# A hybrid decoder block: eight places for the second half's scores, and 72 instead of 68 first-layer blocks ahead of the dense stage

## The chip, the core and the metric

The kernel runs on one core of a Trainium2 chip. Five engines work side by side, each through its own instructions in a fixed order: TensorE (PE), VectorE (DVE), ScalarE (ACT), GpSimd (POOL) and SyncE (SP), which here only issues transfers. The metric is device microseconds of the whole launch.

## The reference, cut to what matters

A decoder block with two token mixers, followed by a retrieval layer (PEER). Only the last part matters here; `x2` is the normalised result of the mixers, 1024 tokens of width 1024.

```python
q = (xb @ w_q).reshape(TOK_BLOCK, PEER_HEADS, 2, PEER_DHALF)
s = jnp.einsum('thcd,hcnd->thcn', q, sub_keys)
top_s, top_i = lax.top_k(s, K)                      # K = 16 of 128, 8 heads x 2 halves
...                                                 # best 16 of the 256 sums per head
e = (i1 * PEER_NKEYS + i2)                          # 128 experts per token, of 16384
gate = jax.nn.softmax(best_s, axis=-1)
act = jax.nn.gelu(jnp.einsum('td,ted->te', xb, expert_u[e]))
return jnp.einsum('te,ted->td', gate * act, expert_v[e])
```

## The kernel before, in words

The 1024 tokens are eight tiles of 128, worked in two halves of four (tiles 0 to 3, then 4 to 7). The mixers are computed for each half in turn; `mix_and_route(hf, ...)` ends each half: it multiplies by `w_o`, normalises, and routes.

**Routing** runs over 16 pieces `m` (8 heads by 2 key halves). For each, PE multiplies `x2` by one tile of `w_q` (24 matmuls into `acc`, named WQ below), ACT copies the result to `qT`, PE forms the scores against the keys (four matmuls into `sc`, L964), ACT copies the scores to SBUF (L966), and DVE takes the 16 best of each token in place (`top16`, L788 to L792). After every fourth piece `route` picks the 16 best pairs of two heads. In the second half the scores' copies go to three buffers (`sc_s`, pool `sq1`), so a fourth copy waits until DVE has done with the first.

**The retrieval** is done in two ways. Tiles 0 to 2, and the first layer of tile 3, are gathered: for each token's 128 experts POOL issues an indirect load of 128 rows of 8 KB (L1002, 1 MB, called a row load below), DVE forms the dot product (L1005), ACT the gate (L1006, L1007), and DVE adds the weighted second part (L997). There are three row buffers (`NROW`). Tile 0's 128 row loads run beside routing and the stage after it, at a low priority; tiles 1 and 2 (256 row loads) run in the dense stage.

For tiles 4 to 7 all 16384 experts are computed, as 128 blocks of 128 experts, and tile 3 joins in for the second layer. This has three stages:

1. `spread_gates` turns indices and gates into a dense table: 160 steps, each three DVE instructions (L1073, L1076, L1083) and one or two of ACT and POOL that build one-hot operands, and four PE matmuls into `pg` (L1085). The last table pieces go to DRAM (`gd`, L1090).
2. First-layer blocks ahead of time: for each block in `PRE`, `u_stage` loads 512 KB of `expert_u`, splits each half into two parts (ACT the high one `uh`, POOL the low one `ul`; four buffers of each), multiplies with 24 matmuls, and ACT applies the gelu into `g1` (L1098), which is stored to DRAM (`gs`, L1232). `g1` has two buffers (pool `up`). `PRE` holds 68 blocks: every even group of four, and the last two groups. PE does these beside stage 1.
3. `dense`: 32 groups of four blocks. For a block in `PRE` the `g1` is loaded back (L1128); for the others (15 odd groups) `u_stage` runs here. DVE multiplies with the gates (L1131), the product is split into `c2`, and for each half of the output columns 60 matmuls (L228 to L230, five token tiles by four blocks by three) accumulate, and DVE adds the result (L1158: ten additions a group). The loop asks for eight rows of tiles 1 and 2 in every group. `vraw` are the 256 KB loads of `expert_v`, split into `vhi` and `vlo`. The first `c2` buffers lie where `spread_gates` had its table pieces `gt`.

The order of instructions on each engine is set by a scheduler when the program is built, with its own estimates of time and with priorities; a stage's instructions may so be interleaved with another's. On the chip each engine keeps that order and waits on semaphores. "U1" to "U72" below are the first-layer blocks in the order of `PRE`.

Of the kernel before, what the change touches and what calls it, by code (L numbers as in the profile page):

```python
# [10 lines left out]
F32 = mybir.dt.float32  # L11
# [9 lines left out]
P = 128  # L21
# [14 lines left out]
WD = 512 + XD  # L36
DT = list(range(4, 8)) + list(range(NGT, 4))
NG, NQ, GB, NB = WD // GT, 512 // GT, 4, 4
PRE = [b for b in range(128) if b // 4 % 2 == 0 or b >= 120]
NROW = 3  # L40
NV2 = 6
SOONER = 300
# [90 lines left out]
def body(tc, a, out):  # L133
# [3 lines left out]
    def pool(es, name, bufs=1, space=None, side=None):  # L137
        kw = {}
        if space is not None:
            kw["space"] = space  # L140
        if side is not None:
            kw["side"] = side
        return es.enter_context(tc.tile_pool(name=name, bufs=bufs, reuse_waits="tile", **kw))
# [649 lines left out]

    def route(tp, hf, hq, tv, ti, F):

# [5 lines left out]
        for i in range(8):  # L801
# [5 lines left out]
        row = cst[:, C_ROW:C_ROW + 16]  # L807
        V.scalar_tensor_tensor(flat(F)[:, :, 1:], tf.rearrange("p t (h x) k -> p (t h) x k", x=2)[:, :, 0], 8192.0,
                               row[:, None, :].to_broadcast([P, 8, 16]), op0=OP.mult, op1=OP.add)
        dF = tp.tile([P, 8, 16], F32, name="dF")  # L810
        V.tensor_sub(dF, flat(F)[:, :, 1:], flat(F)[:, :, :16])
        bv_ = tp.tile([P, 4, 2, 16], F32, name="bv")
# [37 lines left out]
    def mix_and_route(hf, es, xt):  # L850
        side = "right" if hf else None
        if hf == 0:
            xt = pool(es, "xt0")
            mp = pool(es, "mp0")
        if hf:
            sq = pool(es, "sq1", side=side)
            mp = pool(es, "mp1", side=side)
            sp = pool(es, "sp1", side=side)
            mo = pool(es, "mo1", side=side)
        else:  # L860
            sq = sp = pool(es, "sp0")
            mo = mp
        tp = pool(es, f"tp{hf}", 1, side=side)
        if hf == 0:
# [19 lines left out]
        s2 = loaded(mp, sil, "s2", "s2")  # L884
# [65 lines left out]
            SY.dma_start(hd[t], hb[t])  # L950
        subk = mo.tile([P, 16, P], F32, name="subk", tag="o2") if hf else sp.tile([P, 16, P], F32, name="subk")
        SY.dma_start(subk, a["subk"])
        F = tp.tile([P, 4, 2, 17], F32, name="F")
        V.memset(F, 0.0)
        for m in range(16):
            _, hi, lo = wtile(a["w_q"][m], "wq")
            ps = acc_.tile([P, 512], F32, name="acc")
            for c in range(NCD):
                mm3(ps, hi[:, c], lo[:, c], x2[:, 0, c], x2[:, 1, c], c == 0, c == NCD - 1)
            q = sp.tile([P, 512], F32, name="qT", tag="ld", bufs=3)  # L960
            A.activation(q, ps, AF.Copy)
            p2 = sps.tile([P, 4, P], F32, name="sc")
            for t in range(4):
                PE.matmul(p2[:, t], q[:, t * P:(t + 1) * P], subk[:, m], start=True, stop=True)  # L964
            sc = sq.tile([P, 4, P], F32, name="sc_s", bufs=3 if hf else 4)
            A.activation(sc, p2, AF.Copy)  # L966
            if m % 4 == 0:
                tv = tp.tile([P, 4, 4, 16], F32, name="tv", bufs=2)
                ti = tp.tile([P, 4, 4, 16], U32, name="ti", bufs=2)
            for t in range(4):  # L970
                top16(tv[:, t, m % 4], ti[:, t, m % 4], sc[:, t])
            if m % 4 == 3:
                route(tp, hf, m // 4, tv, ti, F)
        return x2
# [126 lines left out]
    def dense(es, x2, gp, hr, direct, gk1, vr):  # L1101
# [14 lines left out]
        for g0 in range(0, P, NB):  # L1116
            blks = range(g0, g0 + NB)
            cs = []
            for b in blks:
# [5 lines left out]
                g1 = up.tile([P, 512], F32, name="g1")  # L1125
                if b in PRE:
                    act = g1
# [69 lines left out]
    with ExitStack() as e0:  # L1197
        mix_and_route(0, e0, None)
# [28 lines left out]
    with ExitStack() as e0:  # L1227
        spread_gates(e0, direct)
    for b in PRE:
        g1 = up.tile([P, 512], F32, name="g1")  # L1230
# [19 lines left out]
```

## Time and profile before

| | |
|---|---|
| median of 3 runs | 3660.15 us (3648.31 to 3672.93) |
| the profiled execution | 3670.3 us, its span 3668.5 us |
| TensorE's mean granted clock | 0.937 of full |
| busy share of the span | PE 90%, DVE 75%, POOL 64%, ACT 42% |
| DMA | 867.64 MB, mean 237 GB/s |

Busy shares are means over stages with different limits. By the trace, the second half's routing lies at about 1595 to 1875 us, the spreading of the gates at 1875 to 2292, and the dense stage at 2313 to 3647; the last outputs are written by 3668. PE's busy time counts pipelined matmuls that overlap, so a count of matmuls says more.

### The profile page before, as it was taken

What the parts mean: (1) busy time and instruction counts of PE and PEld (TensorE: products, weight loads), DVE (VectorE), ACT (ScalarE), POOL (GpSimd) and SP (SyncE); (2) the same over time, 40 slices, a digit from 0 to 9 for tenths busy, and PEclk for the clock granted to TensorE, in tenths of its full rate; (3) what the DMA queues carried; (4) which work ended last, traced back from release to release, by engine and by line L of the source; (5) the groups of instructions that cost most, each with busy time, mean ns of one, the idle gap of its engine ahead of it and who ended that gap; (6) DMA issues with size and microseconds to landing.
All of it is one profiled execution on the core that took longest, in us unless ns stands there. A gap on an engine that the chain in (4) does not pass through costs nothing. (4 is left out here: it accounts for less than half of the span.)

```text
span 3668.5 us, 49271 instructions
## 1 busy us (share of the span) xinstructions
PE 3313.7 (90%) x16175; PEld 2656.0 (72%) x16175; DVE 2738.7 (75%) x5108; ACT 1554.1 (42%) x3711; POOL 2344.6 (64%) x2123
## 2 busy tenths in 40 slices
PE   7999998889888998788889999789999999999996
PEld 7887776677666775576678888567777787777775
DVE  3566538969986777799999999566766666666776
ACT  5555443243344433333346767433333343333333
POOL 3442304536787646755788999666767676776765
PEclk9999969999898897898999999899999999999998
DMA  4321113333677678863589999888888888988986
GB/s 154 110 65 53 55 44 121 106 133 98 206 219 242 189 224 292 312 235 124 186 288 324 326 331 329 318 303 307 325 306 321 326 314 318 326 327 313 336 324 230
DMA packets 347380, 867.64 MB, mean 237 GB/s; under 512 B 53208, under 2 KB 132704, under 8 KB 293876
## 3 DMA queue, kind: packets, MB, share of 16 engines
q0 software_dynamic: 75328, 475.06, 36.5%
q1 hardware_dynamic: 182436, 328.77, 26.8%
q10 hardware_dynamic: 89360, 60.68, 5.2%
q8 instruction: 127, 2.08, 0.2%
q14 instruction: 129, 1.06, 0.1%
HBM read 777.48 MB, written 86.92 MB: 236 GB/s over the span
## 5 line engine op out<-in xcount | busy, mean ns | idle before, releaser
L1002 POOL DMA_INDIRECT row<-euv,idx x384 | 420.7, 1096 | 318.8 <-DVE yr L997 163.5
L1005 DVE SCALAR_TENSOR_TENSOR row<-row,xr 128x1024 f32<-128x1024 f32 x256 | 311.3, 1217 | 166.7 <-DMA row<-euv,idx 164.9
L225 POOL TENSOR_TENSOR vlo<-vraw,vhi 128x512 fp32r<-128x512 f32 x256 | 330.7, 1303 | 149.0 <-ACT vhi L224 129.3
L997 DVE SCALAR_TENSOR_TENSOR yr<-row,act,yr 128x1024 f32<-128x1024 f32 x256 | 329.5, 1287 | 115.5 <-ACT act L1007 109.8
L1006 ACT ACTIVATE act<-act 128x1 f32<-128x1 f32 x384 | 76.8, 200 | 687.4 <-DVE row L1005 683.6
L225 POOL TENSOR_TENSOR ul<-ur,uh 128x512 fp32r<-128x512 f32 x256 | 344.7, 1353 | 36.4 <-ACT uh L224 27.3
L230 PE MATMUL zp<-x,ul 128*128 128x512 f32 x784 | 314.3, 401 | 16.9 <-POOL ul L225 16.9
L228 PE MATMUL py<-vhi,c 128*128 128x512 f32 x640 | 258.9, 409 | 68.2 <-DVE hbuf L1158 31.6
L228 PE MATMUL zp<-x,uh 128*128 128x512 f32 x784 | 314.9, 402 | 0.3 <-ACT g L1098 0.3
L229 PE MATMUL zp<-x,uh 128*128 128x512 f32 x784 | 313.7, 400 | 0.0
L230 PE MATMUL py<-vhi,c 128*128 128x512 f32 x640 | 254.0, 403 | 23.5 <-POOL c L225 23.5
L224 ACT ACTIVATE vhi<-vraw 128x512 fp32r<-128x512 f32 x256 | 159.6, 626 | 256.8 <-DMA vraw<-euv 110.6
L228 PE MATMUL zp<-vhi,c 128*128 128x512 f32 x640 | 249.5, 399 | 12.0 <-DVE hbuf L1158 10.1
L997 DVE SCALAR_TENSOR_TENSOR hr<-row,act,hr 128x1024 f32<-128x1024 f32 x128 | 235.1, 1837 | 33.8 <-ACT act L1007 33.5
L229 PE MATMUL py<-vlo,c 128*128 128x512 f32 x640 | 256.7, 401 | 0.4 <-POOL vlo L225 0.4
L229 PE MATMUL zp<-vlo,c 128*128 128x512 f32 x640 | 250.1, 395 | 0.4 <-POOL vlo L225 0.4
L230 PE MATMUL zp<-vhi,c 128*128 128x512 f32 x640 | 246.8, 395 | 0.0
L349 DVE SCALAR_TENSOR_TENSOR cy<-u,vec,cy 128x512 f32<-128x512 f32 x240 | 241.9, 1008 | 5.4
L1005 DVE SCALAR_TENSOR_TENSOR row<-row,xng 128x1024 f32<-128x1024 f32 x128 | 213.7, 1672 | 16.0 <-DMA row<-euv,idx 16.0
L1024 POOL DMA_INDIRECT row<-euv,twice x128 | 150.3, 1175 | 114.7 <-DVE row L1026 74.1
L1026 DVE SCALAR_TENSOR_TENSOR row<-row,xng 128x1024 f32<-128x1024 f32 x128 | 184.3, 1445 | 51.9 <-DMA row<-euv,twice 51.7
L228 PEld LDWEIGHTS py<-vhi,c 128*128 128x128 f32 x640 | 124.0, 194 | 110.1 <-DVE hbuf L1158 43.2
(1646 smaller groups left out, 9502.0 us busy)
## 6 DMA issues: line engine op xcount, KB each, us to landing
vraw<-euv SPq DMA_DIRECT2D x256, 256.0 KB
ur<-eut SPq DMA_DIRECT2D x256, 256.0 KB
gd<-gt ACTq DMA_DIRECT2D x20, 1920.0 KB
gblk<-gd SPq DMA_DIRECT2D x30, 1280.0 KB
gs<-g SPq DMA_DIRECT2D x68, 256.0 KB
g<-gs SPq DMA_DIRECT2D x68, 256.0 KB
wbr<-w_in SPq DMA_DIRECT2D x64, 256.0 KB
wqr<-w_q SPq DMA_DIRECT2D x64, 256.0 KB
```

Source lines behind the costliest of these rows:

```text
L224: A.activation(hi, src, AF.Copy)
L225: return eng.tensor_sub(lo, src, hi.bitcast(F32))
L228: PE.matmul(ps, whi, xhi, start=first, stop=False)
L229: PE.matmul(ps, whi, xlo, start=False, stop=False)
L230: PE.matmul(ps, wlo, xhi, start=False, stop=last)
L349: V.scalar_tensor_tensor(y, u[:, j:j + 512], cw, y, op0=OP.mult, op1=OP.add)
L997: V.scalar_tensor_tensor(y, row[:, 1], act[:, j:j + 1], y, op0=OP.mult, op1=OP.add)
L1002: G.indirect_dma_start(out=row.rearrange("p a d -> p (a d)"), out_offset=None, in_=a["euv"], in_offset=bass.IndirectOffsetOnAxis(ap=idx[0] ...
L1005: V.scalar_tensor_tensor(row[:, 0], row[:, 0], 1.0, xn, op0=OP.mult, op1=OP.mult, accum_out=aj)
L1006: A.activation(aj, aj, AF.Gelu)
L1024: G.indirect_dma_start(out=row, out_offset=None, in_=a["euv"].rearrange("e (k d) -> (e k) d", k=2), in_offset=bass.IndirectOffsetOnAxis(ap ...
L1026: V.scalar_tensor_tensor(row, row, 1.0, xn, op0=OP.mult, op1=OP.mult, accum_out=act[:, j:j + 1])
```

## The change

The pool `sq1` with its three buffers goes. In the second half the scores' copies go to `scb`, one tile of eight places in the pool `mp1`, under the tag `s2`: the room of the mixers' operand `s2`, which is no longer read at that time (both are 16 KB a partition). Place `m % 8` is used for piece `m`, so a copy waits for DVE's use of the piece eight before it, not three. And `PRE` takes in the blocks 116 to 119 (group 29): 72 blocks run ahead, 56 remain in the dense stage.

```diff
--- before.py
+++ after.py
@@ -36,7 +36,7 @@
 WD = 512 + XD
 DT = list(range(4, 8)) + list(range(NGT, 4))
 NG, NQ, GB, NB = WD // GT, 512 // GT, 4, 4
-PRE = [b for b in range(128) if b // 4 % 2 == 0 or b >= 120]
+PRE = [b for b in range(128) if b // 4 % 2 == 0 or b >= 116]
 NROW = 3
 NV2 = 6
 SOONER = 300
@@ -853,12 +853,11 @@
             xt = pool(es, "xt0")
             mp = pool(es, "mp0")
         if hf:
-            sq = pool(es, "sq1", side=side)
             mp = pool(es, "mp1", side=side)
             sp = pool(es, "sp1", side=side)
             mo = pool(es, "mo1", side=side)
         else:
-            sq = sp = pool(es, "sp0")
+            sp = pool(es, "sp0")
             mo = mp
         tp = pool(es, f"tp{hf}", 1, side=side)
         if hf == 0:
@@ -950,6 +949,7 @@
             SY.dma_start(hd[t], hb[t])
         subk = mo.tile([P, 16, P], F32, name="subk", tag="o2") if hf else sp.tile([P, 16, P], F32, name="subk")
         SY.dma_start(subk, a["subk"])
+        scb = mp.tile([P, 8, 4, P], F32, name="scb", tag="s2") if hf else None
         F = tp.tile([P, 4, 2, 17], F32, name="F")
         V.memset(F, 0.0)
         for m in range(16):
@@ -962,7 +962,7 @@
             p2 = sps.tile([P, 4, P], F32, name="sc")
             for t in range(4):
                 PE.matmul(p2[:, t], q[:, t * P:(t + 1) * P], subk[:, m], start=True, stop=True)
-            sc = sq.tile([P, 4, P], F32, name="sc_s", bufs=3 if hf else 4)
+            sc = scb[:, m % 8] if hf else sp.tile([P, 4, P], F32, name="sc_s", bufs=4)
             A.activation(sc, p2, AF.Copy)
             if m % 4 == 0:
                 tv = tp.tile([P, 4, 4, 16], F32, name="tv", bufs=2)
```

The scheduler makes a new order of the whole second half from this. Three places of it follow.

ACT, second half of routing, before: from the thirteenth score copy (L966) to the fifteenth. `uh` are splits of first-layer weights, `g1` gelus of finished first-layer blocks, `act` the gathered rows' gates.

```order
L966 ACTIVATE sc_s_13873<-sc_13868 128x512
L224 ACTIVATE uh_17762<-ur_17760 128x512
L1098 ACTIVATE g1_17673<-zp_17686 128x512
L224 ACTIVATE uh_17796<-ur_17794 128x512
L224 ACTIVATE uh_17802<-ur_17800 128x512
L1098 ACTIVATE g1_17713<-zp_17726 128x512
L224 ACTIVATE uh_17836<-ur_17834 128x512
L966 ACTIVATE sc_s_13941<-sc_13936 128x512
L224 ACTIVATE uh_17842<-ur_17840 128x512
L1098 ACTIVATE g1_17753<-zp_17766 128x512
L1006 ACTIVATE act_14400<-act_14400 128x1
L966 ACTIVATE sc_s_14007<-sc_14002 128x512
```

The same copies (thirteenth to fifteenth) in the new order, and the sixteenth behind them; `wqh` and `qT` belong to WQ, `bf` to `route`.

```order
L966 ACTIVATE scb_12750<-sc_13854 128x512
L224 ACTIVATE uh_17617<-ur_17615 128x512
L966 ACTIVATE scb_12750<-sc_13921 128x512
L224 ACTIVATE uh_17623<-ur_17621 128x512
L961 ACTIVATE qT_13984<-acc_13959 128x512
L224 ACTIVATE uh_17657<-ur_17655 128x512
L844 ACTIVATE bf_13454<-bf_13454 128x128
L224 ACTIVATE uh_17663<-ur_17661 128x512
L961 ACTIVATE qT_14049<-acc_14024 128x512
L966 ACTIVATE scb_12750<-sc_13986 128x512
L224 ACTIVATE uh_17697<-ur_17695 128x512
L966 ACTIVATE scb_12750<-sc_14051 128x512
```

The last four copies moved ahead of every gelu (L1098) of a first-layer block; before, three of them stand behind one.

DVE, the end of `spread_gates`, before: the last two steps of three instructions, the last row of tile 0 (`hr0`), its final normalisation (L199 to L1039), and the first product of the dense stage (L1131).

```order
L1073 TENSOR_TENSOR o2h_17600<-gT1_17159,keys_15203 128x512
L1076 TENSOR_TENSOR o1h_17602<-gT0_17151,keys_15203 128x256
L1083 TENSOR_SCALAR o1h_17602<-keys_15203,gT0_17151,gT2_17164 128x128
L1073 TENSOR_TENSOR o2h_17614<-gT1_17159,keys_15203 128x512
L1076 TENSOR_TENSOR o1h_17616<-gT0_17151,keys_15203 128x256
L1083 TENSOR_SCALAR o1h_17616<-keys_15203,gT0_17151,gT2_17164 128x128
L997 SCALAR_TENSOR_TENSOR hr0_11908<-row_15163,act_14400,hr0_11908 128x1024
L199 TENSOR_SCALAR rfm_15173<-ssf_15170 128x1
L1131 TENSOR_TENSOR g1_20366<-g1_20366,gblk_15192 128x512
L205 SCALAR_TENSOR_TENSOR rfq_15175<-rfq_15175,rfm_15173 128x1
L206 SCALAR_TENSOR_TENSOR rfr_15176<-rfq_15175,rfr_15176 128x1
L1039 SCALAR_TENSOR_TENSOR sqf_15171<-hr0_11908,rfr_15176,gq_15182 128x1024
```

The same end of `spread_gates` in the new order.

```order
L1073 TENSOR_TENSOR o2h_17595<-gT1_17140,keys_15184 128x512
L1076 TENSOR_TENSOR o1h_17597<-gT0_17132,keys_15184 128x256
L1083 TENSOR_SCALAR o1h_17597<-keys_15184,gT0_17132,gT2_17145 128x128
L1005 SCALAR_TENSOR_TENSOR row_15120,act_14381<-row_15120,xng_14379 128x1024
L997 SCALAR_TENSOR_TENSOR hr0_11908<-row_15120,act_14381,hr0_11908 128x1024
L1005 SCALAR_TENSOR_TENSOR row_15126,act_14381<-row_15126,xng_14379 128x1024
L997 SCALAR_TENSOR_TENSOR hr0_11908<-row_15126,act_14381,hr0_11908 128x1024
L1005 SCALAR_TENSOR_TENSOR row_15132,act_14381<-row_15132,xng_14379 128x1024
L997 SCALAR_TENSOR_TENSOR hr0_11908<-row_15132,act_14381,hr0_11908 128x1024
L1005 SCALAR_TENSOR_TENSOR row_15138,act_14381<-row_15138,xng_14379 128x1024
L997 SCALAR_TENSOR_TENSOR hr0_11908<-row_15138,act_14381,hr0_11908 128x1024
L1005 SCALAR_TENSOR_TENSOR row_15144,act_14381<-row_15144,xng_14379 128x1024
```

Behind the last step there are now five rows of tile 0 (L1005 and L997 each) where there was one L997; in the whole order, 123 rows of tile 0 stand ahead of the last step's first instruction, where there were 128 (L1005).

ACT, from the last gelu to the first `c2`, before: the gelu of U68 stands further up, ahead of the last one-hot operands; here are the normalised rows of tile 1 (`xr`, L993), two rows' gates, and the first splits of the dense stage.

```order
L993 ACTIVATE xr_20405<-xng_20400 128x512 x2
L1006 ACT_TABLE_LOAD
L1006 ACTIVATE act_20402<-act_20402 128x1
L1007 ACTIVATE act_20402<-act_20402,gate0_5953 128x1
L1006 ACTIVATE act_20402<-act_20402 128x1
L1007 ACTIVATE act_20402<-act_20402,gate0_5953 128x1
L224 ACTIVATE c2_20369<-g1_20366 128x512
L224 ACTIVATE c2_20369<-gblk_15192 128x128
L224 ACTIVATE c2_20377<-g1_20374 128x512
L224 ACTIVATE c2_20377<-gblk_15192 128x128
L224 ACTIVATE c2_20385<-gblk_15192 128x128
L224 ACTIVATE vhi_20460<-vraw_20458 128x512
```

In the new order: `uh_20848` and `uh_20854` are the weights of the dense stage's second own block, `g1_20454` is the gelu of U72, the last block ahead, and `c2_20510` the first product of the dense stage.

```order
L224 ACTIVATE uh_20848<-ur_20846 128x512
L224 ACTIVATE uh_20854<-ur_20852 128x512
L993 ACTIVATE xr_20546<-xng_20541 128x512 x2
L1006 ACTIVATE act_20543<-act_20543 128x1
L1007 ACTIVATE act_20543<-act_20543,gate0_5953 128x1
L1006 ACTIVATE act_20543<-act_20543 128x1
L1007 ACTIVATE act_20543<-act_20543,gate0_5953 128x1
L1006 ACTIVATE act_20543<-act_20543 128x1
L1007 ACTIVATE act_20543<-act_20543,gate0_5953 128x1
L1098 ACTIVATE g1_20454<-zp_20467 128x512
L993 ACTIVATE yr_20547<-y0_20544 128x512 x2
L224 ACTIVATE c2_20510<-g1_20507 128x512
```

U72's gelu moved behind two splits, the copies of `xr` and the gates of three rows of tile 1; `c2` follows it.

## Rows read from the trace of the kernel before

**Rows 1.** Busy time by stage; each engine: us busy (instructions); then granted clock, DMA share, GB/s.
```profile
1595.00:1875.00 280.00, 239.44 (x1007) 191.90 (x1006) 278.70 (x995) 93.98 (x202) 187.01 (x120) 0.91 0.53 178
1875.00:2292.00 417.00, 401.51 (x2344) 347.51 (x2342) 408.37 (x654) 286.46 (x772) 382.61 (x306) 1.00 0.99 329
2292.00:2313.00 21.00, 0.00 (x0) 0.00 (x0) 7.34 (x13) 10.00 (x24) 4.73 (x6) 0.54 0.89 307
```

**Rows 2.** Waits of ACT, 1595 to 1755: engine, line, waited for: us, times, longest.
```profile
ACT sc_s L966 <- DVE ti L792: 37.9, 10, 8.8
```

**Rows 3.** Waits of PE, 1595 to 1875.
```profile
PE sc L964 <- ACT sc_s L966: 10.6, 4, 5.1
PE sc L964 <- ACT qT L961: 6.7, 4, 2.8
```

**Rows 4.** Groups by line, 1830 to 2290: count, busy, mean ns, idle before.
```profile
L997 DVE SCALAR_TENSOR_TENSOR hr<-row,act,hr 128x1024 f32<-128x1024 f32 x66 | 128.5, 1947 | 6.1 <-ACT act L1007 6.1
L1005 DVE SCALAR_TENSOR_TENSOR row<-row,xng 128x1024 f32<-128x1024 f32 x65 | 113.2, 1746 | 0.0
```

**Rows 5.** PE in order of time, 2262 to 2400: start, duration, [idle before].
```profile
2267.77 0.39 PE L230 MATMUL zp<-x,ul 128*128 128x512 f32 x1
2272.11 0.40 PE L228 MATMUL zp<-x,uh 128*128 128x512 f32 x1
...
2288.31 3.42 PE L1085 MATMUL pg<-o1h,o2h 128*128 128x128 f32 x24 [1.16 <-ACT o1h L1081]
2313.13 0.79 PE L228 MATMUL py<-vhi,c 128*128 128x512 f32 x1 [21.40 <-ACT vhi L224]
```

**Rows 6.** ACT and its DMA queue in order of time, 2270 to 2400.
```profile
2292.79 0.37 ACTq L1090 DMA_DIRECT2D gd<-gt  x1
2298.84 1.23 ACT L993 ACTIVATE xr<-xng 128x512 f32<-128x512 f32 x2 [2.42 <-DMA xng<-xg]
...
2301.39 0.20 ACT L1006 ACTIVATE act<-act 128x1 f32<-128x1 f32 x1
2301.62 0.29 ACT L1007 ACTIVATE act<-act,gate 128x1 f32<-128x1 f32 x1
...
2311.53 0.63 ACT L224 ACTIVATE c<-g 128x512 fp32r<-128x512 f32 x1 [7.77 <-DMA gd<-gt]
```

**Rows 7.** SP's queue in order of time, 2220 to 2400.
```profile
2281.94 4.85 SPq L1128 DMA_DIRECT2D g<-gs  x2
...
2304.95 8.90 SPq L1128 DMA_DIRECT2D g<-gs  x2
```

**Rows 8.** POOL in order of time, 2260 to 2400.
```profile
2303.64 1.28 POOL L225 TENSOR_TENSOR c<-g,c 128x512 fp32r<-128x512 f32 x1 [2.71 <-ACT c L224]
```

**Rows 9.** DVE in order of time, 2270 to 2400.
```profile
2301.25 1.22 DVE L1005 SCALAR_TENSOR_TENSOR row<-row,xr 128x1024 f32<-128x1024 f32 x1
...
2311.15 0.69 DVE L1131 TENSOR_TENSOR g<-g,gblk 128x512 f32<-128x512 f32 x1 [0.57 <-DMA g<-gs]
...
2326.31 0.69 DVE L1158 TENSOR_TENSOR hbuf<-hbuf,py 128x512 f32<-128x512 f32 x1 [6.42 <-PE py L230]
...
2348.91 0.68 DVE L1158 TENSOR_TENSOR hr<-hr,zp 128x512 f32<-128x512 f32 x1
```

**Rows 10.** Busy time by stage, groups 27 to 31 of the dense stage.
```profile
3453.90:3501.50 47.60, 47.51 (x209) 38.79 (x208) 35.99 (x49) 20.93 (x53) 36.82 (x35) 1.00 0.94 342
3501.50:3535.00 33.50, 31.37 (x135) 24.83 (x134) 22.61 (x31) 8.92 (x26) 23.43 (x24) 1.00 0.90 321
3535.00:3584.80 49.80, 48.03 (x204) 39.08 (x203) 38.95 (x52) 19.92 (x53) 34.32 (x34) 0.97 0.90 329
3584.80:3617.30 32.50, 29.82 (x128) 23.52 (x127) 27.20 (x36) 11.16 (x32) 24.45 (x24) 1.00 0.90 311
3617.30:3646.60 29.30, 25.82 (x111) 20.23 (x109) 21.21 (x28) 15.31 (x41) 12.53 (x12) 1.00 0.50 178
```

**Rows 11.** DMA, 2350 to 3640: the stretch's packets, bytes and mean rate.
```profile
DMA packets 100828, 411.12 MB, mean 319 GB/s; under 512 B 11200, under 2 KB 11200, under 8 KB 65344
```


## The prediction

> **What bounds the kernel now.** I read the stages first, then the waits in the stage that the new places touch, then the two joints that the new order moves. From 1595 to 1875 us, where the second half is routed, DVE is busy 278.7 of 280 us while PE is busy 239.4 [rows 1]: DVE is the bound, and whatever waits for it there gives no time back unless DVE itself gets less to do. The score copies do wait: ACT stands 37.9 us for DVE's use of the old buffers, and PE 17.3 us for the copies and for `qT` [rows 2, 3]. From 1875 to 2292, the spreading of the gates, DVE is busy 408 of 417 us, PE 402, and the transfers stand at a share of 0.99 [rows 1]: three resources are full at once. Then PE does nothing for 21.4 us, until 2313.1 [rows 5]. The cause is not what the page names first: ACT waits 7.8 us for the last table piece on its way to DRAM, issued at 2292.8 and gone by 2311.5 [rows 6], since `c2` lies where that piece lay, and the splits `vhi` stand behind it on ACT. In the dense stage a group with its own first layer takes about 50 us and a group from `PRE` about 33 [rows 10].
>
> **The places.** They take away the copies' waits. Both orders have the same DVE work up to the end of routing, except that the new one has three rows of tile 0 fewer ahead of its last index; so PE's 17.3 us [rows 3] buy only an earlier stand of PE, which then waits for DVE at the fourth step of the spreading. The saving of the places by themselves is nothing; the cover is DVE's full 280 us. If DVE had gaps there, it could be up to 17 us.
>
> **Rows of tile 0 behind the spreading.** What does move DVE's end is that five L1005 and four L997 now stand behind the last step. At 1.746 and 1.947 us [rows 4] that is 8.7 + 7.8 = 16.5 us that DVE has not to do before it. Is PE able to follow? At the fourth step the old order has 23.6 first-layer blocks behind it, the new one 22.6; up to the last step 44.4 and 43.0 follow. A matmul of a block takes 0.2284 us (19 steps in 4.34 us [rows 5]), a block of 24 then 5.5 us; PE so has 7.6 us less to do within the spreading, and the earlier start (three rows, 11 us) is covered by the 17.3 us of waits. DVE says 16 us earlier, PE 18; I take **-16** for the last `pg`. Bounds: -8, if the transfers, which are as full and lose little, hold it, and -18.
>
> **The four more blocks, at the joint.** In the new order six whole blocks and nine matmuls of a seventh stand between the last `pg` and the first matmul of the dense stage: 153 x 0.2284 = **35 us** of PE where there were 21.4 us of nothing. The piece on its way to DRAM (18.7 us) is hidden by that. But a new chain begins at U72. The first `g1` of the dense stage needs one of the two buffers that the last blocks use, and the load stands on SP behind U72's store. U72's gelu stands on ACT behind `uh_20854`, whose buffer (one of four) is free only when U72's last high product is done, then behind `xr` and the gates of three rows of tile 1, each waiting for its L1005. From U72's end: split 0.6, `xr` 1.2 [rows 6], three dot products 3.7 [rows 9], the last gate 0.5 [rows 6], gelu 0.6: 6.6 to 7.2 us. Then store and load: the old third load came between 2304.95 and 2311.15 [rows 7, 9], 6.2 us; the two after one another took 8.9 us to issue, so 3 to 6 us. Then product 0.7 [rows 9], split 0.6 [rows 6], low part 1.3 [rows 8]. So PE's first product after about 15 us, and, since each further block needs the `g1` buffer of one before, 4 us for each of the other three and 2.7 us of matmuls for the last: 15 + 12 + 2.7 = 29.5 us from U72's end to the first sums. Before, it was 2291.7 to 2326.3 [rows 5, 9], 34.6 us; now 35 + 29.5 = 64.5: **+30**. Bounds: +20, if the loads land in 3 us and the blocks overlap, and +45, if the loads of the last blocks, tile 1's rows and the table piece crowd each other (share 0.89 even in the empty stretch [rows 1]).
>
> Behind the first sums, the second half of group 0 took 2326.3 to 2349.6, 23.3 us [rows 9], of which 16.5 us are 72 matmuls; it waited for `vraw`. In the new order six `vhi` are split ahead of U72's end, so I take **-3** (0 to -6).
>
> **The dense stage.** Group 29 becomes a group without its own first layer: 49.8 us before, against 33.5, 32.5 and 29.3 of its neighbours [rows 10], so -17. Its row loads do not go away: before, L1005 counts 10, 6, 12, 7 and 4 in groups 27 to 31, now 12, 6, 5, 7 and 5, with three more done by the first sums; so group 27 should take some 2 us more. Together **-15**. Bounds: -22, all 96 matmuls, and -3, if only the transfer counts: the group loads 2 MB less and reads back 1 MB, and 1 MB at 319 GB/s [rows 11] is 3 us. I take the value near the neighbours' rows, since those groups have the same eight row loads asked for.
>
> Sum: -16 + 30 - 3 - 15 = **-4 us** against the profiled execution's 3670.3. That run lies 10 us above the median 3660.15, within the spread of the three runs; against the median it is 3656. Up to 1595 the order changes in single places of the mixers' last stage only (s2 is split earlier, rows stand elsewhere, the count ahead of routing is the same); I price that at 0, with 5 us either way.
>
> **Rivals.**
>
> *The dense stage is held by its transfers, and group 29 gives nothing.* Place: groups 27 to 31. For it: 319 GB/s through the whole stage [rows 11], a share of 0.85 to 0.94 where row loads still come [rows 10], and groups from `PRE` that need 33 us for 120 matmuls, which at 0.2284 are 27.4. Against it: a group with 96 matmuls more takes 17 us more, though it loads only a little more, and it gets more rows done. It decides if four `PRE` groups in a row cannot pull their rows faster than about one in 5 us. Then -3 in place of -15, and with the upper half of the joint's price: +8 to +20, 3668 to 3680, **slower**, most likely 3673.
>
> The Trainium skill ("Perfetto Trace Analysis", Identifying the Most-Contended Engine and Engine Utilization) judges PE by the busy share of its weight loads and the transfers by the share of a peak of 358 GB/s per core. In group 29 the weight loads are busy 39.1 of 49.8 us, 78% [rows 10], and 319 of 358 GB/s [rows 11] is 89%. By that rule the transfers are the bound, not PE, and this rival would be the forecast; the trace does not agree for the single group, whose length follows its matmuls.
>
> *The joint costs almost nothing.* U72's gelu is soon done, loads land in 3 us, and the routing's 17 us count in part: -18 + 20 - 6 - 20 - 5 = -29, 3631. For it: in the empty stretch nothing but the table piece and two loads were awaited. Against it: U72's gelu cannot pass the rows of tile 1 in ACT's order.
>
> *The rows at the joint come late.* After the last step DVE has eight L1005 ahead of the first product, the last three of tile 1; with three row buffers and 10 us from issue to use under load, the third of tile 1 could come 20 us after U72's end. Then the joint costs 50 to 60 us, not 30, the dense stage gives back little, and the time is 3690 to 3700.
>
> **How the numbers follow.** The forecast, a sum between -14 and +6, has 0.55; held by transfers 0.2; the cheap joint 0.17; late rows 0.08. One per cent, 36.6 us, is about what a measurement of this kernel can tell from no change. Only the tail of the cheap joint lies below -1% (0.06), only late rows lie near or above +1% (0.07); 0.87 between. The range leaves out late rows and the cheap joint's tail: 3630 to 3682.
>
> **What would show it.** Right: in 1595 to 1800 no wait of ACT's score copies for DVE, and DVE as full as before; the last `pg` at about 2275; first-layer matmuls to about 2311, then a gap of PE of 10 to 18 us that ends on `c2` or a load of `g1`; first sum at about 2340; group 29 at 30 to 35 us. Wrong: DVE with idle time in routing (the places count); U67 to U72 with gaps for `ul` or `ur` (transfers crowd the joint); groups 28 to 31 at 38 us or more each (transfers hold the end).

## The result, and the profile after

The changed kernel takes 3692.6 us (median of 18 runs; 3662.3 for the kernel before on the same chip): the ratio is **1.0068, 95% interval 1.0048 to 1.0088**, some 25 us slower. Two of the 18 runs took 4547 and 5249 us, at a granted clock of 0.64 and 0.55; the ratio leaves them out. The profiled execution takes 3695.0 us, its span 3693.2 us, against 3670.3 and 3668.5 before.

The stages of [rows 1] in the changed kernel (same columns; the last line is the stretch from the last `pg` to the first matmul of the dense stage):

```profile
1595.00:1875.00 280.00, 230.10 (x1009) 184.86 (x1009) 276.88 (x985) 90.73 (x196) 182.30 (x116) 0.92 0.52 174
1875.00:2278.00 403.00, 385.40 (x2272) 333.36 (x2272) 394.84 (x640) 279.40 (x756) 379.65 (x297) 1.00 0.97 324
2278.00:2346.00 68.00, 40.55 (x154) 32.09 (x152) 24.76 (x25) 27.58 (x58) 36.48 (x30) 0.79 0.80 279
```

DVE is as full in routing as it was. ACT's wait of [rows 2] is gone, and PE's waits of [rows 3] have changed place, not size. Waits of ACT, 1595 to 1755 us, and of PE, 1595 to 1875, the two longest of each:

```profile
ACT bf L844 <- DVE bf L843: 33.3, 3, 16.3
ACT act L1006 <- DVE row L1005: 31.2, 8, 6.1
```

```profile
PE sc L964 <- ACT qT L961: 19.3, 5, 10.0
PE zp L228 <- ACT g L1098: 9.3, 5, 5.0
```

The joint, against [rows 5 and 9]: PE in order of time, the last piece of `pg` and then every matmul ahead of which PE stood still for over 2 us; and DVE's first addition.

```profile
2275.92 1.95 PE L1085 MATMUL pg<-o1h,o2h 128*128 128x128 f32 x16
...
2308.65 0.79 PE L228 MATMUL zp<-x,uh 128*128 128x512 f32 x1 [12.41 <-ACT g L1098]
...
2325.35 0.80 PE L228 MATMUL zp<-x,uh 128*128 128x512 f32 x1 [2.97 <-ACT g L1098]
...
2345.87 0.80 PE L228 MATMUL py<-vhi,c 128*128 128x512 f32 x1 [12.07 <-ACT c L224]
```

```profile
2360.28 0.68 DVE L1158 TENSOR_TENSOR hbuf<-hbuf,py 128x512 f32<-128x512 f32 x1
```

The last `pg` ends at 2277.9, 13.8 us earlier than before. But the first addition comes 82.4 us behind it, where it was 34.6. PE's first stop is new. ACT in order of time, against [rows 6]:

```profile
2306.45 1.67 ACT L224 ACTIVATE vhi<-vraw 128x512 fp32r<-128x512 f32 x3 [11.28 <-DMA gd<-gt]
2308.02 0.58 ACT L1098 ACTIVATE g<-zp 128x512 f32<-128x512 f32 x1
...
2318.49 1.28 ACT L202 ACT_TABLE_LOAD   x1
...
2324.70 0.60 ACT L1098 ACTIVATE g<-zp 128x512 f32<-128x512 f32 x1
...
2339.43 0.58 ACT L1098 ACTIVATE g<-zp 128x512 f32<-128x512 f32 x1
```

Three `vhi` of the dense stage stand ahead of a gelu in ACT's order, and wait 11.3 us for the table piece, whose room they take. By the count of gelus it is U68's (2308.0). U70 is the block that stops: PE writes first-layer blocks to two banks in turn (`zps`, two buffers), so U70's first matmul (2308.65) waits for U68's gelu. Some expectations below call it "U70's gelu"; U70's own (2324.7) comes behind tile 0's normalisation and its table loads (`ACT_TABLE_LOAD`), and is what U72 waits for. The piece was issued at 2278.5 and is gone 27.9 us later (18.7 before). SP waits for it too: its wait from 2278 on, and what the transfers do in 2290 to 2310 (40 slices: busy tenths, GB/s):

```profile
SPq L234 <- DMA gd<-gt: 13.7, 1, 13.7
```

```profile
DMA  9999998999999999999999990111100000059936
GB/s 381 388 443 442 438 421 367 460 411 326 410 433 382 373 385 356 348 349 375 435 455 403 445 378 16 52 52 52 36 20 22 23 2 0 0 164 365 393 131 205
```

Groups 28, 29 and 31 of the dense stage, against [rows 10]: group 29 has become 14.8 us shorter, the end 2.3 us longer.

```profile
3538.00:3572.30 34.30, 30.75 (x131) 23.98 (x131) 24.61 (x33) 11.12 (x32) 23.18 (x23) 1.00 0.88 313
3572.30:3607.30 35.00, 31.34 (x125) 23.75 (x124) 22.25 (x32) 9.75 (x26) 23.98 (x24) 0.95 0.81 301
...
3639.70:3671.30 31.60, 27.11 (x116) 21.26 (x115) 23.58 (x30) 15.87 (x43) 14.83 (x14) 1.00 0.56 201
```

| term | forecast | measured in the two profiles |
|---|---|---|
| last `pg` (2291.7) | -16 | -13.8 |
| last `pg` to first sums (34.6) | +30 | **+47.8** |
| first sums to the end of group 0 (23.3) | -3 | -3.2 |
| groups 1 to 31 (1297.0) | -15 | -6.2 |
| sum | -4 | +24.6 |

The last `pg` is earlier in part because work left its stage: 57 first-layer matmuls of the old blocks (13 us) now stand behind it, beside the 96 of the four new ones.

### The profile page after: what moved, and what is told of

Its sections match the earlier page's. It is cut to its first block, busy times and chain, and to the rows that moved or that the text cites. A ratio compares the mean times of both kernels' runs of the same rounds, so it can differ in the third digit from the quotient of the medians.

```text
span 3693.2 us, 49309 instructions
## 1 busy us (share of the span) xinstructions
PE 3305.2 (89%) x16175; PEld 2646.0 (72%) x16175; DVE 2762.2 (75%) x5108; ACT 1552.4 (42%) x3709; POOL 2358.9 (64%) x2123
## 5 line engine op out<-in xcount | busy, mean ns | idle before, releaser
L1002 POOL DMA_INDIRECT row<-euv,idx x384 | 432.2, 1126 | 295.7 <-DVE yr L997 155.0
L1005 DVE SCALAR_TENSOR_TENSOR row<-row,xr 128x1024 f32<-128x1024 f32 x256 | 311.4, 1217 | 161.1 <-DMA row<-euv,idx 147.0
L997 DVE SCALAR_TENSOR_TENSOR yr<-row,act,yr 128x1024 f32<-128x1024 f32 x256 | 329.4, 1287 | 117.3 <-ACT act L1007 112.4
L228 PE MATMUL zp<-x,uh 128*128 128x512 f32 x800 | 323.7, 405 | 24.7 <-ACT g L1098 24.7
L230 PE MATMUL zp<-x,ul 128*128 128x512 f32 x800 | 324.5, 406 | 8.9 <-POOL ul L225 8.9
L229 PE MATMUL zp<-x,uh 128*128 128x512 f32 x800 | 322.3, 403 | 0.0
L997 DVE SCALAR_TENSOR_TENSOR hr<-row,act,hr 128x1024 f32<-128x1024 f32 x128 | 233.7, 1826 | 43.3 <-ACT act L1007 43.0
L1005 DVE SCALAR_TENSOR_TENSOR row<-row,xng 128x1024 f32<-128x1024 f32 x128 | 226.4, 1770 | 15.3 <-DMA row<-euv,idx 15.0
L1026 DVE SCALAR_TENSOR_TENSOR row<-row,xng 128x1024 f32<-128x1024 f32 x128 | 185.5, 1455 | 58.0 <-DMA row<-euv,twice 57.8
L224 ACT ACTIVATE uh<-ur 128x512 fp32r<-128x512 f32 x256 | 159.0, 624 | 111.5 <-PE zp L229 63.9
```

The costliest lines, as they stand in the source:

```text
L224: A.activation(hi, src, AF.Copy)
L228: PE.matmul(ps, whi, xhi, start=first, stop=False)
L229: PE.matmul(ps, whi, xlo, start=False, stop=False)
L230: PE.matmul(ps, wlo, xhi, start=False, stop=last)
L997: V.scalar_tensor_tensor(y, row[:, 1], act[:, j:j + 1], y, op0=OP.mult, op1=OP.add)
L1002: G.indirect_dma_start(out=row.rearrange("p a d -> p (a d)"), out_offset=None, in_=a["euv"], in_offset=bass.IndirectOffsetOnAxis(ap=idx[0] ...
```

## The experiments

Ratios are against the kernel before on the same chip, with 95% intervals. "Joint" is the time from the last `pg` to the first addition, from the profile. A profile is one execution of one build: in kernels with the same work there (the order differs), groups 2 to 26 took between 1047 and 1083 us, so a dense stage that differs by 10 or 20 us tells nothing. The joint is steadier: 29.2 to 36.2 us in the kernels that leave it as it was before.

**The two parts apart.** e1_places is the changed kernel with 68 blocks; e2_blocks is the kernel before with 72.

```diff
-PRE = [b for b in range(128) if b // 4 % 2 == 0 or b >= 116]
+PRE = [b for b in range(128) if b // 4 % 2 == 0 or b >= 120]
```

> The eight places alone, 68 blocks ahead as before. Theory (the loss lies at the joint, and only where the added blocks stand there): the last pg comes 12 to 16 us earlier than before, as in the changed kernel, since fewer rows of tile 0 stand ahead of it. The splits vhi stand in ACT's order ahead of U68's gelu, behind the table piece on its way to DRAM, but only one block's gelu waits there, so PE loses at most its stop before the dense stage: first sums 0 to 12 us earlier than before. Time -12 to 0 us against the kernel before, most likely -5 (ratio 0.9986). Rival (the places and the new order cost time by themselves): ratio 1.004 or more, the last pg no earlier or routing longer than 280 us.

> Four more blocks ahead, the scores in three buffers as before. In this order vhi stand ahead of U72's gelu alone, not ahead of U70's. Theory: the table piece leaves while U69 to U72 run, PE does not stop for a gelu as it did in the changed kernel (12.4 us), the joint from the last pg to the first sums takes 60 to 72 us (82.4 in the changed kernel, 34.6 before), the last pg comes as before (2285 to 2295), the dense stage gives 6 to 12 us. Time +10 to +25 us against the kernel before, most likely +18 (ratio 1.005). Rival (transfers crowd the joint, the order on ACT is of no matter): joint 80 us or more, time +30 to +45 (ratio 1.008 to 1.012).

The places alone are slower: 1.0051 (1.0027 to 1.0076). Routing did not get longer; the last `pg` came 12.6 us earlier, and the joint took 59.8 us, 25.2 more than before. Of these, 13 us are 57 first-layer matmuls that stood ahead of the last `pg` before, and 5.6 us are PE's longer stop (27.0 in place of 21.4). Here is PE's stop in it (in order of time), on the wait of `vhi` for the table piece and then on tile 0's normalisation:

```profile
2318.97 0.80 PE L228 MATMUL py<-vhi,c 128*128 128x512 f32 x1 [26.98 <-ACT c L224]
```

The blocks alone: 1.0075 (1.0047 to 1.0103), joint 53.9 us, less than expected, and yet slower than expected. So neither part is harmless, and the two losses, +19 and +27 us, don't add up to more than +25. The theories had both too cheap.

**Closing the joint's ways.** e3_vhi_behind and e4_group0_behind change ACT's order by an edge behind U72's gelu (`ahead`), for `vhi` or for all of ACT's work in the first group. e8_pool_queue moves the last piece off the queue whose later transfers wait for it, e9_pool_queue_behind does both e4 and e8, and e7_piece_early takes that piece away (the last lines). Below are the edits of e3, e8 and e7, shortened.

```diff
+                    with tc.issue_after(ahead) if g0 == 0 else ExitStack():
-                    split(hi, lo, raw)
+                        split(hi, lo, raw)
...
-                A.dma_start(gd[k:, :, P // GT * s_ + g].rearrange("k p x -> p k x"),
+                (G if tt == max(DT) and g == P // GT - 1 else A).dma_start(gd[k:, :, P // GT * s_ + g].rearrange("k p x -> p k x"),
...
+                if tt == max(DT) and g == P // GT - 2:
+                    A.dma_start(slot(g + 1), piece)
```

> The changed kernel, with the splits vhi of the dense stage's first group put behind U72's gelu in ACT's order; nothing else is asked for. Theory (ACT's order lets U70's gelu wait for the table piece): PE's stop of 12.4 us goes, and most of the 2.6 us of slow matmuls after it; joint 64 to 72 us in place of 82.4; time -9 to -16 us against the changed kernel, most likely -12, so +13 us against before (ratio 1.0035). Rival (transfers crowd the joint: PE would wait for ur or uh instead): joint above 78 us, time within 4 us of the changed kernel (ratio 1.006 to 1.008).

> The changed kernel, with all of ACT's work of the dense stage's first group (vhi, c2, xr, yr, the gates of the first rows of tile 1) behind U72's gelu. Theory: as with vhi alone, and U72's gelu no longer waits for tile 1's first dot products, some 5 us more; joint 60 to 68 us; tile 1's first rows come some 5 us later, which the dense stage pays back in part. Time -12 to -20 us against the changed kernel, most likely -15 (ratio 1.0025 against before). Rival (transfers crowd the joint): joint above 78 us, ratio 1.006 to 1.008.

> The changed kernel, with the very last table piece's own write to DRAM left out; in its place the piece before it is written twice (so 16 tokens of a tile get other tokens' gates). The bytes written are the same, but nothing waits behind the last pg for a piece of 19 to 28 us. Theory (that piece holds ACT, whose vhi splits wait for its room, and SP, whose transfers wait for it, and through both the gelus of U70 to U72): PE stops for no gelu by more than 4 us in the joint, joint 55 to 64 us in place of 82.4, time -18 to -27 us against the changed kernel, ratio 0.9995 to 1.002 against before. Rival (U72's own chain, i.e. tile 0's normalisation, tile 1's first rows, gelu, store, load, sets the first sums whatever the piece does): joint above 74 us, ratio 1.0045 to 1.0075.

> The changed kernel, with the last table piece issued on POOL's queue in place of ACT's; ACT's order is as in the changed kernel. Theory: SP no longer waits for the piece (12 to 14 us there), but vhi still stand ahead of U70's gelu and wait for its room; PE's stop of 12 us for U70's gelu stays, the later ones shrink. Joint 74 to 82 us, time 0 to -7 us against the changed kernel (ratio 1.005 to 1.007). Rival (the wait on SP is what counts): joint 60 to 68 us, ratio 1.000 to 1.003.

> Both mends: the last table piece on POOL's queue, and all of ACT's work of the dense stage's first group behind U72's gelu. Theory (two ways lead from the piece to the gelus, over ACT's order and over SP's; with only one closed, 8 us of stop stayed): PE runs U67 to U72 with no stop above 3 us; joint 60 to 66 us; time -15 to -22 us against the changed kernel, ratio 1.001 to 1.003. Rival (transfers crowd the joint in any order): PE waits for uh or ul, joint above 70 us, ratio 1.006 or more.

| kernel | joint | ratio |
|---|---|---|
| the change | 82.4 | 1.0068 (1.0048 to 1.0088) |
| e3_vhi_behind | 74.0 | 1.0101 (1.0059 to 1.0144) |
| e4_group0_behind | 72.3 | 1.0091 (1.0062 to 1.0120) |
| e7_piece_early | 73.2 | 1.0081 (1.0052 to 1.0110) |
| e8_pool_queue | 72.7 | 1.0028 (0.9998 to 1.0059) |
| e9_pool_queue_behind | 71.6 | 1.0040 (1.0010 to 1.0071) |

Each takes 8 to 11 us off the joint, and none reaches 66; in none of the five does a theory or its rival have both the joint and the ratio right. e3, e4 and e7 are no faster than the change. The two with the piece on POOL's queue are lower (1.0028 and 1.0040): e8 gives back some 15 of the 25 us, and on the same chip its runs lie 17 us on average (8 to 25) below e7's, at the same joint. In e8 the `vhi` wait 1.9 us for the piece, which is gone 16.5 us after its issue, so the long stop that its theory had asked to stay is not there:

```profile
2295.29 1.67 ACT L224 ACTIVATE vhi<-vraw 128x512 fp32r<-128x512 f32 x3 [1.86 <-DMA gd<-gt]
```

PE's waits in the joint of e9, where no instruction ahead of a gelu waits for the piece, and PE's wait for a gelu in that of e4:

```profile
PE py L228 <- ACT c L224: 12.6, 1, 12.6
PE zp L228 <- ACT g L1100: 6.9, 2, 5.9
```

```profile
PE zp L228 <- ACT g L1100: 7.8, 1, 7.8
```

The gelus (here L1100) now stand behind the gates of tile 0's last rows, whose loads come late, and behind tile 0's normalisation with its table loads (in e4 the last 2.8 us are a wait for the store of an earlier `g1`). So the theory is right on what stops PE, for some 10 us, and wrong on what holds the time: in e3, e4 and e7 the time did not fall with the joint. Why it fell in e8, by more than the joint did, is open.

**What a group's first layer is worth in the dense stage.** Left out there are the 96 matmuls of group 29 (e5_no29), or those of five groups (e12_less5); the stored `g1` of other blocks are loaded instead.

```diff
-                if b in PRE:
+                if b in PRE or b // 4 in (21, 23, 25, 27, 29):
                     act = g1
-                    SY.dma_start(g1, gs[b])
+                    SY.dma_start(g1, gs[b if b in PRE else b - 4])
```

> The kernel before, with the first layer of group 29 left out of the dense stage: its four blocks load the stored g1 of group 28 again. Nothing is added at the joint. Theory (a group's length follows its matmuls; what the four blocks save in the dense stage is 12 to 18 us): group 29 takes 32 to 36 us in place of 49.8, time -15 us against the kernel before (ratio 0.996). Rival (the dense stage is held by its transfers, and row loads make the neighbours longer by what group 29 saves): groups 27 to 31 together shorter by less than 5 us, ratio 0.999 to 1.001.

> The kernel before, with the first layer of five groups (21, 23, 25, 27, 29) left out of the dense stage: their 20 blocks load the stored g1 of the group before. Theory A (a group's length follows its matmuls, and so does the stage): time -60 to -80 us against the kernel before, ratio 0.978 to 0.984. Theory B (the 256 row loads need some 5 us each with three buffers, and so hold the dense stage as a whole; what PE saves is then spent waiting, or rows are left over behind the last group): time -10 to +5 us, ratio 0.997 to 1.001.

e5: group 29 took 34.5 us, and the time stayed: 1.0005 (0.9974 to 1.0036), which leaves out the theory's 0.996. The rival's way is not seen either: groups 27 to 31 together got 11 us shorter, not less than 5; what took these back, one profile doesn't tell. e12: 480 matmuls less are 110 us of PE at the spacing of [rows 5], and the time fell by 19 us: 0.9949 (0.9924 to 0.9973), between the two theories and nearer B. Its groups did get shorter (groups 1 to 31 took 1198.6 us in place of 1297.0); but the row loads were not done by then. The stretch behind its last group, in the columns of [rows 1], 96.3 us where there were 22.6, and no matmul in it:

```profile
3547.30:3643.60 96.30, 0.00 (x0) 0.00 (x0) 65.96 (x86) 23.38 (x65) 28.35 (x25) 0.51 0.80 293
```

**Bytes without work.** e13_norows2 leaves out 126 rows of tile 2; e14_tables leaves out 15 loads of gate tables (those groups use the table of the group before); e15_more_loads adds 60 loads that are overwritten.

```diff
-            for j in range(P):
+            for j in range(P if tt < NGT - 1 else 2):
...
-                elif b % GB == 0:
+                elif b % GB == 0 and b // GB % 2:
...
                 else:
+                    SY.dma_start(g1, gs[b // 8 * 8])
                     act = u_stage(b, None, x2, bank())
```

> The kernel before, with 126 of tile 2's 128 rows left out (loads, dot products, gates and sums), so that the second half of the dense stage has no row loads. Theory B (row loads hold the stage): groups 17 to 31 fall from 645 us to 590 to 610 us, near their 2592 matmuls at 0.2284 us (592 us), and a group from PRE takes 27 to 29 us. Theory A (matmuls alone set a group's length): groups 17 to 31 take 630 to 645 us, a group from PRE 31 us or more.

> The kernel before, with every second load of a gates' table (1.31 MB each, 15 of 30, those of the even groups) left out of the dense stage; these groups use the table of the group before. No instruction of PE, DVE, ACT or POOL is taken away. Theory T (from the end of routing on the transfers hold the time, at some 318 GB/s in the dense stage): 19.7 MB less are 62 us; a group from PRE falls from 33.6 us to 28 to 30, ratio 0.983 to 0.988. Rival (the chain of row load, dot product and addition on DVE holds it, by waiting and not by bytes): a group from PRE stays above 32 us, ratio 0.995 to 1.000.

> The kernel before, with 60 needless loads of 256 KB in the dense stage: each block of an own group loads a stored g1 first, which its own product then overwrites. Theory T (transfers hold): 15.7 MB more are 49 us; +25 to +50 us, ratio 1.007 to 1.014, with the mean rate of the dense stage at 312 to 320 GB/s as before. Rival (own groups are held by their 216 matmuls alone): +8 us or less, ratio 1.000 to 1.002.

e13 is 0.9882 (0.9840 to 0.9923). The 645 us and 2592 matmuls of its expectation are those of groups 16 to 31; these took 606 us (645.8 before), as theory B said. Without row loads every group stands at its matmuls; here an own group and one from `PRE`:

```profile
3380.00:3429.20 49.20, 49.11 (x215) 40.08 (x215) 11.46 (x17) 13.52 (x27) 27.99 (x25) 1.00 0.37 118
3429.20:3457.10 27.90, 27.90 (x124) 22.95 (x123) 7.18 (x11) 9.47 (x19) 16.65 (x15) 1.00 0.40 133
```

So an own group, some 50 us with its rows too, is held by PE; a group from `PRE`, 29 to 40 us with rows (groups 2 to 30 before), is not. 126 row loads are 132 MB, yet the time falls by no more than 43 us: PE is the next limit. e14: 0.9879 (0.9843 to 0.9916), -44 us, where theory T's bytes were 62 and its ratio 0.983 to 0.988; a group from `PRE` fell to 31.9 us on average (groups 2 to 26; 35.0 before), which is neither theory's number. e15: 1.0104 (1.0075 to 1.0134), +38 us, as T said; in its profile the stretch behind the last group is 22.6 us longer, where leftover rows are done. An added load also stands ahead of its block's product in the same buffer, but PE's waits for `c` in the dense stage stayed (15 us in both). The dense stage's transfers (from the end of group 0 to that of group 31; before, e14, e15):

```profile
DMA packets 100848, 411.28 MB, mean 317 GB/s; under 512 B 11200, under 2 KB 11200, under 8 KB 65344
```

```profile
DMA packets 98846, 392.21 MB, mean 314 GB/s; under 512 B 10978, under 2 KB 10978, under 8 KB 65257
```

```profile
DMA packets 108081, 418.86 MB, mean 322 GB/s; under 512 B 12001, under 2 KB 12001, under 8 KB 73445
```

The rate stays within 314 to 322 GB/s while the bytes change by 27 MB.

**The places' rows.** e16_rows0 is e1_places without tile 0's last five rows.

```diff
-            for j in range(P):
+            for j in range(P - 5 if rp is None else P):
```

> The eight places alone (68 blocks), with the last five rows of tile 0 left out (loads, dot products, gates and sums). In that order they are what stands between the last step of the spreading and the joint's end on DVE and ACT. Theory T (the places cost nothing in routing; the five rows come back at the joint with 5 MB of transfers and with their gates ahead of the last gelu): first sums 38 to 48 us behind the last pg (59.8 with them), time -12 to -18 us against the places with all rows, ratio 1.0000 to 1.0025 against before. Rival (the table piece on its way to DRAM and ACT's order hold the joint, rows or not): 55 us or more, ratio 1.004 to 1.006.

1.0018 (0.9994 to 1.0043), as theory T said, 12 us below e1; its joint took 52.4 us, between the two expectations, since PE's stop ahead of `c` is still 21.5 us. By the two ratios the five rows are most of the places' loss, though the intervals overlap. The run takes away their work (18 us of DVE by [rows 4], 5 MB) and not only their place, and no run leaves them out of the kernel before; so how much of the 12 us is due to the place stays open.

**Other sets of blocks.** e10_swap and e11_swap_places run group 29 ahead in place of group 0, whose first layer falls into the joint; e17_64 takes group 31 back into the dense stage, e18_no0 group 0.

```diff
+PRE = [b for b in range(128) if (b // 4 % 2 == 0 and b >= 4) or b >= 116]
...
+PRE = [b for b in range(128) if b // 4 % 2 == 0]
...
+PRE = [b for b in range(128) if (b // 4 % 2 == 0 and b >= 4) or b >= 120]
```

> The kernel before with 68 blocks ahead, but other ones: group 29's four blocks in place of group 0's. Group 0's first layer then runs in the dense stage itself, i.e. in the empty stretch at the joint, with no store and load of g1 and with its gelus ahead of the splits in ACT's order. Theory (at the joint PE has 21 us of nothing that 22 us of matmuls can fill, if nothing of them stands behind the table piece; group 29 then is 15 us shorter, but the row loads, which are spread over the groups, end up to 8 us later): first sums 36 to 44 us behind the last pg (34.6 before), time -5 us against the kernel before (-14 to +4; ratio 0.9985). Rival (the dense stage is held by its row loads: what group 29 saves is lost to them): ratio 1.000 to 1.004.

> The same 68 blocks (group 29 in place of group 0) with the eight places for the scores. Theory: the last pg 12 to 14 us earlier, but tile 0's last rows, their gates and its normalisation stand among the joint's gelus on ACT, and vhi ahead of one of them: first sums 55 to 68 us behind the last pg; time 0 to +12 us against the kernel before (ratio 1.0015). Rival (the joint is cheap once no store and load of g1 stands in it): first sums 45 us or less behind the last pg, ratio 0.996 or less.

> The kernel before with 64 blocks ahead (group 31's four back in the dense stage): the other direction of the change's second half. 2.1 MB less of stores and loads of g1 are 6.6 us at 318 GB/s. Theory T (the bytes behind routing hold the time): -3 to -10 us, ratio 0.997 to 0.999. Rival (PE's matmuls hold it: 96 more at the end, where no row loads are left to pull): group 31 takes 45 to 50 us in place of 29.3, +10 to +20 us, ratio 1.003 to 1.005.

> The kernel before with 64 blocks ahead, group 0's four run in the dense stage itself, in the empty stretch at the joint. 2.1 MB less of stores and loads, and 96 matmuls where PE had nothing to do. Theory T: first sums 32 to 40 us behind the last pg, dense stage as before, time -4 to -12 us, ratio 0.9965 to 0.999. Rival (what the joint takes in, the groups behind it give back, as with group 29 in place of group 0): ratio 1.001 to 1.005.

e10: joint 33.7 us with group 0's first layer in it, for no more than an empty one took, and yet 1.0050 (1.0025 to 1.0075); what the joint took in, the stages behind it gave back. e11: joint 59.4 us, 1.0106 (1.0069 to 1.0143), more than either theory: its rows end late, 39.4 us behind the last addition where there were 22.6. e17: 1.0067 (1.0035 to 1.0099). Group 31 took 49.6 us, with no rows left to pull beside its matmuls:

```profile
3606.10:3655.70 49.60, 48.72 (x213) 39.50 (x211) 26.58 (x38) 22.21 (x55) 21.84 (x21) 1.00 0.42 152
```

So theory T by itself falls there: 2 MB less didn't help, and 96 matmuls more cost all of their 22 us. e18: 0.9985 (0.9955 to 1.0016), no difference that can be told. No version that does all the work was measurably faster than the kernel before.

## Why the prediction was wrong

**What held.** The places give nothing in routing: DVE stayed full (276.9 of 280 us). The last `pg` came 13.8 us earlier (forecast 16). The last gap of PE was 12.1 us and ended on `c2` (10 to 18). U72's own chain, from its last matmul (2333.8) to the first sums, took 26.5 us (29.5). The second half of group 0 gave 3.2 us (3).

**The step that failed** is "The four more blocks, at the joint": +30, with an upper bound of +45, measured +47.8. Its 35 us for U67 to U72 took 55.9 (2277.9 to 2333.8): 35 of matmuls, 15.4 of two stops for gelus, and 5 more because some 13 matmuls behind each stop stood 0.43 us apart in place of 0.23. "The piece on its way to DRAM (18.7 us) is hidden by that" was wrong: the blocks have gelus, and three splits that wait for the piece stand ahead of U68's, for whose bank U70 waits. I had looked at what stands ahead of U72's gelu only. The mends show 8 to 11 us for this way and the one over SP. Some 7 us of stops stayed in them (e4 7.8, e9 6.9), behind tile 0's gates and normalisation on ACT. I booked the five rows behind the last step as a gain of 16 us there, but charged them nowhere at the joint. The gain itself is in good part no gain: in e1 the last `pg` came 12.6 us earlier, but 13 us of matmuls moved behind it, and the joint lost 25.2. Without the five rows (e16) 12 of e1's 19 us were gone, by the two ratios.

**The second term that failed** is the dense stage: -15, measured -6 in one profile. By the whole kernel's time it is worth nothing that can be measured (e5: 1.0005). That was the first rival, "held by its transfers", to which I gave 0.2; with +48 at the joint in place of its upper half comes the measured time. But the sign that I had named for it, groups 28 to 31 at 38 us or more, did not come (31.6 to 35.0); so its price held and its place did not. (I read a share of 0.85 to 0.94 off [rows 10] for it; it is 0.90 to 0.94.) My reason against it, that a group's length follows its matmuls, is true of a group and false of the stage: the row loads of tiles 1 and 2 must be done as well, and come behind the last group if the groups get shorter (e12).

**A rival that hit by luck.** "The rows at the joint come late" names 3690 to 3700 us, and the measured time lies there. Its way did not happen: tile 1's first three rows were worked from 2335.4 to 2338.9 one after another, and DVE had waited there for `xr` from ACT, not for a row load.

**What holds the time.** From the first step of the spreading (1797.8 before, 1768.7 after) to the end, the transfers moved, before and after:

```profile
DMA packets 217005, 585.58 MB, mean 313 GB/s; under 512 B 15861, under 2 KB 92661, under 8 KB 171642
```

```profile
DMA packets 220848, 596.30 MB, mean 310 GB/s; under 512 B 16288, under 2 KB 93088, under 8 KB 174880
```

The spreading begins 29 us sooner (routing itself, whose end overlaps with it, computes its last index at 1871.0 in place of 1875.0), but 10.7 MB more are moved from there on, 34 us at 313 GB/s: 2.1 MB are the four blocks' way to DRAM and back, and the rest row loads and weights that had been moved beside routing, where the transfers are busy half the time [rows 1]. That is +5 us; the other 20 are the lower rate (596.30 MB would take 1905 us at 313 GB/s, they took 1924.5). Most of that lies ahead of the last `pg`, and little at the joint (286 GB/s in 82.4 us, 268 in 34.6 before); from the first step of the spreading to the last `pg`, before and after:

```profile
1797.80:2291.70 493.90, 463.90 (x2592) 397.29 (x2590) 484.27 (x761) 312.53 (x836) 448.45 (x344) 0.98 0.94 314
```

```profile
1768.70:2277.90 509.20, 471.31 (x2630) 400.58 (x2629) 498.02 (x814) 315.53 (x841) 468.69 (x349) 0.98 0.91 305
```

This account is arithmetic on two profiles and shows no cause by itself. e14 (-44 for 19.7 MB) and e15 (+38 for 15.7 MB) show that bytes without any work cost some 0.7 of their price at that rate. But e17 shows that PE's matmuls cost all of theirs where no row loads are left, and e13 that 132 MB less give no more than 43 us. Shown, then, is a stage in which both are nearly full: more bytes cost most of their price, more matmuls at its end theirs, and fewer matmuls give a sixth (e12). Not shown is how the change's 25 us divide between the joint and the transfers: e3, e4 and e7 shorten the joint and give nothing, e8 gives 15 us, and e10 is slower than before at an equal joint. The spread of single profiles is as large as these.

The Trainium skill ("Perfetto Trace Analysis", Identifying the Most-Contended Engine and Engine Utilization) has one improve the most contended resource, and compares the transfers by their rate with 358 GB/s per core; 317 GB/s in the dense stage is 89% of that. By that rule the rival was the forecast, as I had noted; e5, e12 and e14 agree, e17 doesn't, for the last group alone.

## What to carry to other kernels

Work that an order pushes out of a stage is not gone: charge it, its loads and its place in each queue where it lands, and ask which resource is full there. A stage of alternating groups can be held by PE in one kind and by transfers in the other; a group that gets shorter then proves nothing for the stage. Leaving work out without its bytes, and bytes without their work, tells which of the two a stage would pay for. And a stop that is mended in the trace is not yet time: ask the whole kernel's time for it.

## What was not expected of the hardware

- The last table piece (1.97 MB) took 27.9 us, though in its last 4 us (2302 to 2306.4) the transfers moved 2 to 52 GB/s in all (above). Issued on POOL's queue (e8) it took 16.5 us; one execution each, and the cause is open. A load of `ur` (issued by SP at 2306.5) waited 13.7 us for it without sharing any data with it: in the trace the transfers of SP's and ACT's queues take eight semaphores in turn, and the load had the one of the piece. With the piece on POOL's queue SP had no such wait.
- In 2278 to 2346 the granted clock was 0.79 on average. Behind each of PE's three stops (12.4, 3.0 and 12.1 us) it was 0.50, and some 13 matmuls stood 0.43 us apart in place of 0.23: some 2.6 us lost each time.
